# Half-width seven-product gate blocks in a two-layer transformer trunk: what one change does to its time

## The chip, the cores and the metric

The kernel runs on one core of one Trainium2 chip. The metric is the device time of one execution in microseconds (us). The engines named here are TensorE (PE: matrix products, with PEld for its weight loads), VectorE (DVE), ScalarE (ACT), GpSimd (POOL) and SyncE (SP, which issues the DMAs).

## The reference

256 tokens of width 2048 pass through two post-norm layers: layer 0 mixes by two kinds of 128-wide attention heads, layer 1 by latent attention. Each layer ends with a SwiGLU block of inner width 5632, which is where the change is:

```python
def swiglu(x, w_gate, w_up, w_down):
    return (jax.nn.silu(x @ w_gate) * (x @ w_up)) @ w_down
...
x = layer_norm(DEEPNORM_ALPHA * x + y, ln_g[layer, 0], ln_b[layer, 0])
y = swiglu(x, ffn_w_gate[layer], ffn_w_up[layer], ffn_w_down[layer])
```

All inputs and the output are float32.

## The kernel before, in words

**Products.** Every large product keeps float32 accuracy by splitting both factors into a high and a low part of type fp32r. `mm3` (L96) makes one product from three matmuls: high by high (L97), high by low weights (L98), low by high weights (L99). The activations are the stationary factor (128 rows of the contraction by 128 tokens), the weights are streamed, up to 512 columns to a matmul. Transposed activations lie in `XH`/`XL` (input of a product) and `YH`/`YL` (input of the output and down projections).

**Chunks, visits, pieces.** A *chunk* is an output block of 256 tokens by 512 columns; it sums in two PSUM banks, one for each half `t` of the tokens. A *piece* is 256 rows of the weights of one chunk (two contraction tiles `kk`), 512 KB. A *visit* is the use of one piece: `emit_visit` (L277) issues 2 `kk` x 2 `t` x 3 = 12 matmuls of 512 columns. The program is a list of visits built ahead by `kmajor`, `lead_begin`, `lead_end` and `ffn_part` (L177).

**Order of the work.** Every engine runs its own instructions in the order of the program text. For each visit the text issues the matmuls, then the evacuation of a finished chunk (`done`), then hooks tied to that visit (`at`), and then `feed_more` (L269).

**The feeder.** `feed_dma` (L231) issues the DMA of a piece into one of `NRAW` = 5 buffers `raw` on SP. `feed_split` (L244) makes its high part `wh` on ACT (L261) and its low part `wl = raw - wh` on DVE (L262), into one of `NW` = 9 pairs of buffers. A pair comes free at the last visit of its piece, so after each visit the split of the piece nine places on is issued; ACT waits there for PE to end the visit, DVE waits for ACT, and the `raw` buffer that comes free lets SP fetch another piece.

**FFN of a layer.** Eleven blocks `f` of 512 inner columns, in three groups (3, 4, 4 blocks). For each block the gate chunk `g` and the up chunk `u` (8 visits each). `g_done` (L758): Silu on ACT. `u_done` (L762): product on DVE. `h_T` (L765): four PE transposes for each half of the tokens, split into `YH`/`YL`. After a group, four down chunks `d`, each added to the residual on DVE (`residual`, L602). PSUM: four banks for chunks (`mm`), two for attention and some half chunks (`att`), two for transposes (`tp`).

**Between the mixer and the FFN** `setup_ln` (L707) runs the layer norm on DVE, ACT and POOL. The last chunk of the mixer and the first gate chunk visit five of their pieces one half of the tokens at a time to cover this. In layer 0 `toeplitz_prep` (L468) writes a bias table `t_d` of 1.5 MB on the same SP queue as the weights.

Of the kernel before, what the change touches and what calls it, by code (L numbers as in the profile page):

```python
# [9 lines left out]
F32 = mybir.dt.float32  # L10
# [11 lines left out]
NRAW = 5  # L22
NW = 9
# [10 lines left out]
class Chunk:  # L34
    """One GEMM output block: 2 token tiles x n columns, contracted over kt k-tiles."""

    def __init__(self, name, xs, kslots, subs, src, tags=("mm",)):
        self.name = name
        self.xs = xs
        self.kslots = kslots  # L40
        self.subs = subs
        self.src = src
        self.tags = tags
        self.nh = len(kslots) // 2
        self.n = sum(n for n, _ in subs) if subs else 0
        self.ps = {}
        self.subs_t, self.tags_t = {}, {}
        self.done = None


@with_exitstack
def trunk_kernel(ctx: ExitStack, tc: tile.TileContext, x, ab_w_in, b_f, ab_w_out,
# [35 lines left out]
    def ptile(tag):  # L88
        return psum.tile([P, 512], F32, name=uid(tag), tag=tag,
                         bufs={"mm": 4, "att": 2, "tp": 2}[tag])  # L90
# [10 lines left out]
    # ---------------------------------------------------------------- program  # L101
# [73 lines left out]
    GROUPS = ((0, 1, 2), (3, 4, 5, 6), (7, 8, 9, 10))  # L175

    def ffn_part(layer):  # L177
        for gi, grp in enumerate(GROUPS):
            for f in grp:
                for nm, w in (("g", w_gate), ("u", w_up)):  # L180
                    c = add_chunk(f"{nm}{layer}_{f}", "X", K16, ([512], lambda h, w=w, f=f: rows(
                        w[layer], h * 256, [(0, 512, f * 512)])))
                    if f == 0 and nm == "g":
                        lead_begin(c)
                    else:
                        kmajor(c)
            for n in range(4):
                c = add_chunk(f"d{layer}_{gi}_{n}", "Y", list(range(4 * len(grp))), (
                    [512], lambda h, b=grp[0] * 512, n=n: rows(
                        w_down[layer], b + h * 256, [(0, 512, n * 512)])))  # L190
                if gi == 2 and n == 3:
                    (lead_final if layer == 1 else lead_end)(c)
                else:
                    kmajor(c)

# [24 lines left out]
    # ----------------------------------------------------------------- feeder  # L220
# [8 lines left out]
    raws, wts = {}, {}  # L229

    def feed_dma(j, halves=False):  # L231
        if j >= len(pieces):
            return
        c, h = pieces[j]
        r = feed.tile([P, HPMAX], F32, name=uid("raw"), tag="raw", bufs=NRAW)
# [6 lines left out]
    whole = {}  # L242

    def feed_split(j, halves=False, part=None):  # L244
        if j >= len(pieces):
            return
        c, h = pieces[j]
        n = 2 * c.n
        if part != 1:
            r = raws.pop(j)  # L250
            wh = feed.tile([P, HPMAX], F32R, name=uid("wh"), tag="wh", bufs=NW)
            wl = feed.tile([P, HPMAX], F32R, name=uid("wl"), tag="wl", bufs=NW)
            wts[j] = (wh[:, :n].rearrange("p (k c) -> p k c", k=2),
                      wl[:, :n].rearrange("p (k c) -> p k c", k=2))
            whole[j] = (r, wh, wl)
        r, wh, wl = whole[j]
        cuts = [(0, c.n), (c.n, n)] if halves or part is not None else [(0, n)]
        if part is not None:
            cuts = [cuts[part]]
        for a, b in cuts:  # L260
            nc.scalar.activation(wh[:, a:b], r[:, a:b], AF.Copy)  # L261
            nc.vector.tensor_tensor(wl[:, a:b], r[:, a:b], wh[:, a:b].bitcast(F32),  # L262
                                    op=ALU.subtract)
        if part != 0:
            whole.pop(j)

    fs = {}

    def feed_more(lim):  # L269
        while fs["nsp"] < min(lim, len(pieces)):  # L270
            feed_split(fs["nsp"])
            fs["nsp"] += 1
            while fs["nd"] < len(pieces) and fs["nd"] - fs["nsp"] < NRAW:
                feed_dma(fs["nd"])
                fs["nd"] += 1

    def emit_visit(i):  # L277
        c, h, toks, *half = visits[i]
        j = pid[c.name, h]
# [16 lines left out]
    # ----------------------------------------------------- attention chains  # L296
# [57 lines left out]
    def transposes_r(srcs):  # L354
        tp = psum.tile([P, 512], F32R, name=uid("tpr"), tag="tp", bufs=2)
# [73 lines left out]
    # ------------------------------------------------------------- layer 0  # L429
# [143 lines left out]
    # --------------------------------------------------------- layer norm, FFN  # L573
    ff = {}

    def open_ffn(layer, src):
# [17 lines left out]
        at((f"{pre}2", 6, (0, 1)), lambda: load_b(layer, 0))  # L594

# [111 lines left out]
    def setup_ln(c3, nxt, final=False):  # L707
        """c3: chunk completing the sum; nxt: first chunk that reads the result."""
# [19 lines left out]
        def split_a():  # L728
            assert fs["nsp"] == p0 + 4
            feed_split(p0 + 4, part=0)  # L730
            fs["nsp"] += 1
# [20 lines left out]
    def ffn_done(layer):  # L752
        for gi, grp in enumerate(GROUPS):
            for li, f in enumerate(grp):
                cg, cu = chunks[f"g{layer}_{f}"], chunks[f"u{layer}_{f}"]
                hs = {}

                def g_done(t, cg=cg, hs=hs):  # L758
                    hs[t] = ff["pool"].tile([P, 512], F32, name=uid("s"), tag="s", bufs=4)
                    nc.scalar.activation(hs[t], cg.ps[t][0], AF.Silu)  # L760

                def u_done(t, cu=cu, hs=hs):  # L762
                    nc.vector.tensor_tensor(hs[t], hs[t], cu.ps[t][0], op=ALU.mult)

                def h_T(t, hs=hs, li=li):  # L765
                    tp = transposes([hs[t][:, k * P:(k + 1) * P] for k in range(4)])
                    sl = (slice(None), slice(4 * li, 4 * li + 4), slice(t * P, (t + 1) * P))
                    hilo(YH[sl], YL[sl], tp.rearrange("p (k c) -> p k c", k=4))

                cg.done, cu.done = g_done, u_done  # L770
                nx = (f"g{layer}_{f + 1}" if li + 1 < len(grp) else f"d{layer}_{gi}_0")
                at((nx, 1, (0, 1)), lambda h_T=h_T: h_T(0))
                at((nx, 2, (0, 1)), lambda h_T=h_T: h_T(1))
            for n in range(4):
                c = chunks[f"d{layer}_{gi}_{n}"]
                c.done = lambda t, half=None, c=c, n=n, gi=gi: residual(
                    c.ps[t], t, n, gi == 0, gi == 2,
                    fine=(layer == 1 and gi == 2 and t == 1), half=half)
# [6 lines left out]
    at(("u0_1", 0, (0, 1)), lambda: load_g(0, 1))  # L785
    at(("u0_1", 4, (0, 1)), lambda: load_b(0, 1))
# [5 lines left out]
    setup_ln(chunks["d0_2_3"], chunks["m0"])  # L792
# [4 lines left out]
    at(("m0", LEAD + 1, (0, 1)), lambda: (close_pool("ffn"), open_mla()))  # L797
    setup_ln(chunks["om3"], chunks["g1_0"])
    at(("u1_1", 0, (0, 1)), lambda: load_g(1, 1))
    at(("u1_1", 4, (0, 1)), lambda: load_b(1, 1))  # L800
    setup_ln(chunks["d1_2_3"], None, final=True)

    # ------------------------------------------------------------- layer 1
# [80 lines left out]
    for h in (5, 6, 7):  # L884
        hold["m2", h, (0, 1)] = pid["m2", 4] + NW + 1
# [90 lines left out]
    # ------------------------------------------------------------- emission  # L976
# [17 lines left out]
    warm = psum.tile([P, 512], F32, name="warm", tag="tp", bufs=2)  # L994
# [23 lines left out]
    for i, (c, h, toks, *half) in enumerate(visits):  # L1018
# [21 lines left out]
        if last_use[c.name, h] == i:  # L1040
            j = pid[c.name, h]
            if c.name == "v0" and h in (0, 2, 4):
                x_T(h + 2)
                feed_more(h + 3)
                x_T(h + 3)
            feed_more(min(j + NW + 1, i + 3 if i <= 4 else 8 + 17 * (i - 4) // 10, hold.get((c.name, h, toks), 10 ** 6)))
# [13 lines left out]
        if (c.name in ("oa1", "om1") and h == 6):  # L1060
            assert not chains, [(ch["head"], ch["stage"]) for ch in chains]
    close_pool("ffn")
# [57 lines left out]
```

## Time and profile before

| what | value |
|---|---|
| three runs | 2221.16, 2221.16, 2222.12 us; median 2221.16 us |
| span of the profiled execution | 2216.2 us (no other time is shown for it) |
| PE busy | 2182.8 us, 98% of the span |
| DVE, ACT, POOL busy | 1199.6 us (54%), 959.5 us (43%), 93.2 us (4%) |
| moved by DMA | 408.50 MB, mean 184 GB/s |

The span goes from the first to the last instruction of the profiled execution; the time of a run also holds what lies around it. Busy times of PE are those of overlapping instructions, so the pace of matmuls is read from the starts of one and the next.

### The profile page before, as it was taken

What the parts mean: (1) busy time and instruction counts of PE and PEld (TensorE: products, weight loads), DVE (VectorE), ACT (ScalarE), POOL (GpSimd) and SP (SyncE); (2) the same over time, 40 slices, a digit from 0 to 9 for tenths busy, and PEclk for the clock granted to TensorE, in tenths of its full rate; (3) what the DMA queues carried; (4) which work ended last, traced back from release to release, by engine and by line L of the source; (5) the groups of instructions that cost most, each with busy time, mean ns of one, the idle gap of its engine ahead of it and who ended that gap; (6) DMA issues with size and microseconds to landing.
All of it is one profiled execution on the core that took longest, in us unless ns stands there. A gap on an engine that the chain in (4) does not pass through costs nothing.

```text
span 2216.2 us, 26462 instructions
## 1 busy us (share of the span) xinstructions
PE 2182.8 (98%) x10134; PEld 1788.7 (81%) x10134; DVE 1199.6 (54%) x1443; ACT 959.5 (43%) x1232; POOL 93.2 (4%) x142
## 2 busy tenths in 40 slices
PE   9989999999999999999999999999999999999997
PEld 8768888888888888888888898888888888888886
DVE  6545556664544445445456677575454445444455
ACT  5444544354334443344433676344434443344441
POOL 2100000100000000000001321010000000000000
PEclk9989999999999999999999999999999999999999
DMA  8565655576566656666554644756565655665552
GB/s 286 136 185 153 180 173 188 182 239 224 184 188 188 182 181 189 190 184 187 180 184 148 207 127 134 265 172 226 180 189 183 187 183 187 186 188 181 189 184 74
DMA packets 229672, 408.50 MB, mean 184 GB/s; under 512 B 13961, under 2 KB 58025, under 8 KB 228521
## 3 DMA queue, kind: packets, MB, share of 16 engines
q1 hardware_dynamic: 229544, 406.81, 58.7%
q8 instruction: 79, 1.29, 0.2%
q14 instruction: 49, 0.39, 0.0%
HBM read 400.99 MB, written 5.77 MB: 184 GB/s over the span
## 4 chain that ended last, share of the span: by engine, by line
PE 96%; DMA 1%; DVE 1%; POOL 0%; ACT 0%; issue 0%; SPq 0%; DVEq 0%; ACTq 0%; POOLq 0%
PE mm L97 30%; PE mm L99 30%; PE mm L98 30%; PE tp L351 3%; DMA raw<-in_ab_w_in_dram 1%; PE att L98 1%; PE att L99 1%; PE att L97 1%; DVE X L669 0%; DVE X L663 0%; DMA xb<-in_x_dram 0%; ACT wh L261 0%; PE att L948 0%; PE att L949 0%; PE att L547 0%
## 5 line engine op out<-in xcount | busy, mean ns | idle before, releaser
L262 DVE TENSOR_TENSOR wl<-raw,wh 128x1024 fp32r<-128x1024 f32 (+3 forms) x748 | 899.1, 1206 | 814.8 <-ACT wh L261 810.8
L261 ACT ACTIVATE wh<-raw 128x1024 fp32r<-128x1024 f32 (+3 forms) x748 | 776.4, 1041 | 899.4 <-PE mm L99 830.2
L97 PE MATMUL mm<-wh,XH 128*128 128x512 f32 (+3 forms) x1984 | 785.6, 396 | 0.0
L99 PE MATMUL mm<-wh,XL 128*128 128x512 f32 (+3 forms) x1984 | 775.8, 391 | 0.0
L98 PE MATMUL mm<-wl,XH 128*128 128x512 f32 (+3 forms) x1984 | 773.8, 390 | 0.0
L99 PEld LDWEIGHTS mm<-wh,XL 128*128 128x128 f32 x1984 | 373.2, 188 | 84.4
L98 PEld LDWEIGHTS mm<-wl,XH 128*128 128x128 f32 x1984 | 373.9, 188 | 79.9
L97 PEld LDWEIGHTS mm<-wh,XH 128*128 128x128 f32 x1984 | 373.7, 188 | 79.4 <-ACT wh L261 0.2
L97 PE MATMUL mm<-wh,YH 128*128 128x512 f32 x960 | 380.1, 396 | 0.0
L99 PE MATMUL mm<-wh,YL 128*128 128x512 f32 x960 | 378.1, 394 | 0.0
L98 PE MATMUL mm<-wl,YH 128*128 128x512 f32 x960 | 377.0, 393 | 0.0
L99 PEld LDWEIGHTS mm<-wh,YL 128*128 128x128 f32 x960 | 180.2, 188 | 42.8
L98 PEld LDWEIGHTS mm<-wl,YH 128*128 128x128 f32 x960 | 180.4, 188 | 41.7
L97 PEld LDWEIGHTS mm<-wh,YH 128*128 128x128 f32 x960 | 180.4, 188 | 40.9
L658 POOL TENSOR_TENSOR mv<-mv,neghalf 128x1 f32<-128x1 f32 x8 | 7.6, 951 | 1832.1 <-DVE mv L657 1832.1
L93 ACT ACTIVATE YH<-tp 128x512 fp32r<-128x512 f32 x44 | 26.3, 598 | 85.0 <-PE tp L351 85.0
L94 DVE TENSOR_TENSOR YL<-tp,YH 128x512 fp32r<-128x512 f32 x44 | 30.4, 691 | 57.4 <-ACT YH L93 57.4
L93 ACT ACTIVATE XH<-tp 128x512 fp32r<-128x512 f32 x36 | 21.5, 597 | 72.5 <-PE tp L351 72.4
L760 ACT ACTIVATE s<-mm 128x512 f32<-128x512 f32 x44 | 26.1, 598 | 22.9 <-PE mm L99 20.7
L378 ACT ACTIVATE P<-P,sm 128x128 f32<-128x128 f32 x64 | 28.6, 449 | 16.7 <-DVE sm L368 16.7
L93 ACT ACTIVATE qkh<-tp 128x512 fp32r<-128x512 f32 x32 | 18.7, 597 | 37.7 <-PE tp L351 37.7
L94 DVE TENSOR_TENSOR qkl<-tp,qkh 128x512 fp32r<-128x512 f32 x32 | 21.7, 689 | 18.7 <-ACT qkh L93 18.7
(165 smaller groups left out, 962.3 us busy)
## 6 DMA issues: line engine op xcount, KB each, us to landing
raw<-in_ffn_w_gate_dram SPq DMA_DIRECT2D x176, 512.0 KB, 3.9
raw<-in_ffn_w_up_dram SPq DMA_DIRECT2D x176, 512.0 KB, 3.6
raw<-in_ffn_w_down_dram SPq DMA_DIRECT2D x176, 512.0 KB, 4.5
raw<-in_ab_w_in_dram SPq DMA_DIRECT2D x128, 256.0 KB, 3.2
raw<-in_ab_w_out_dram SPq DMA_DIRECT2D x32, 512.0 KB, 3.7
raw<-in_mla_w_out_dram SPq DMA_DIRECT2D x32, 512.0 KB, 3.9
raw<-in_ab_w_in_dram SPq DMA_DIRECT2D x24, 512.0 KB, 3.9
raw<-in_mla_w_ukv_dram SPq DMA_DIRECT2D x16, 512.0 KB, 3.6
```

The costliest lines, as they stand in the source:

```text
L93: nc.scalar.activation(hi, src, AF.Copy)
L94: nc.vector.tensor_tensor(lo, src, hi.bitcast(F32), op=ALU.subtract)
L97: nc.tensor.matmul(o, lh, rh, start=start, stop=False)
L98: nc.tensor.matmul(o, lh, rl, start=False, stop=False)
L99: nc.tensor.matmul(o, ll, rh, start=False, stop=stop)
L261: nc.scalar.activation(wh[:, a:b], r[:, a:b], AF.Copy)
L262: nc.vector.tensor_tensor(wl[:, a:b], r[:, a:b], wh[:, a:b].bitcast(F32), op=ALU.subtract)
L351: nc.tensor.transpose(tp[:, i * P:(i + 1) * P], s_, ident)
L378: nc.scalar.activation(pt[:, a:b], pt[:, a:b], AF.Exp, bias=sm[:, 2 + q:3 + q], accum_out=sm[:, 4 + q:5 + q])
L658: nc.gpsimd.tensor_tensor(mv[:, 3:4], mv[:, 2:3], neghalf, op=ALU.pow)
L760: nc.scalar.activation(hs[t], cg.ps[t][0], AF.Silu)
```

## The change

It touches the FFN of both layers, the feeder and the use of PSUM. Gates 1 to 10 of each layer become "S" chunks: their two halves of tokens, two contraction tiles of a piece and two halves of columns form a 2 x 2 by 2 x 2 block product, computed as seven block products of 128 x 128 by 128 x 256 in place of eight (a Strassen-Winograd scheme). Sums of activation blocks are made once per layer (`xs_batch`, four batches, into tiles `XS`); sums of weight blocks are made for each piece (`split_s`) in an enlarged raw buffer; the four results are put together when a gate chunk ends (`drain_s`). Gate 0 stays as it was.

```diff
-NRAW = 5
-NW = 9
+NR, NW = 4, 4
...
+    def s_window(on):
+        rot["mm"] = [0, 1, 7] if on else [0, 1, 2, 3]
+        rot["tp"] = [6] if on else [6, 7]
...
-    GROUPS = ((0, 1, 2), (3, 4, 5, 6), (7, 8, 9, 10))
+    GROUPS = ((0, 1), (2, 3), (4, 5), (6, 7), (8, 9, 10))
...
+        lead_begin(wide("g", w_gate, 0))
+        base = len(visits)
+        for f in range(NF):
+            kmajor(wide("u", w_up, f))
+            if f in (2, 4, 6, 8):
+                down(f // 2 - 1)
+        down(len(GROUPS) - 1)
+        flat = visits[base:]
...
+        for k, v in enumerate(flat):
+            visits.append(v)
+            want = (k - 3) * 0.85 if k < 22 else 16 + (k - 22) * 0.52
+            while ns < min(len(gates), want):
+                visits.append(gates[ns])
+                ns += 1
...
+    raw_free = [("N", feed.tile([P, HPMAX], F32, name=f"raw{i}")) for i in range(NR)]
+    raw_free += [("S", feed.tile([P, 2048], F32, name=f"sraw{i}")) for i in range(2)]
+    w_free = [("N", (feed.tile([P, HPMAX], F32R, name=f"wh{i}"),
+                     feed.tile([P, HPMAX], F32R, name=f"wl{i}"))) for i in range(NW)]
+    w_free += [("S", (feed.tile([P, 1792], F32R, name=f"sh{i}"),
+                      feed.tile([P, 1792], F32R, name=f"sl{i}"))) for i in range(2)]
...
+    def pay(keep=None):
+        for k, fn in list(owed):
+            if k != keep:
+                fn()
+        owed[:] = [x for x in owed if x[0] == keep]
+
+    def split_s(j):
+        r = raws.pop(j)
+        sh, sl = slot_of[j][1]
+        v = r.rearrange("p (q c) -> p q c", c=256)
+        nc.vector.tensor_tensor(v[:, 4:6], v[:, 0:1].broadcast_to([P, 2, 256]), v[:, 1:3],
+                                op=ALU.subtract)
+        nc.vector.tensor_tensor(v[:, 6], v[:, 1], v[:, 5], op=ALU.subtract)
+        nc.vector.tensor_tensor(v[:, 7], v[:, 3], v[:, 6], op=ALU.subtract)
+        nc.scalar.activation(sh, r[:, 256:2048], AF.Copy)
+
+        def lo():
+            nc.vector.tensor_tensor(sl, r[:, 256:2048], sh.bitcast(F32), op=ALU.subtract)
+            raw_free.append(rslot_of.pop(j))
...
+        owed.append((j, lo))
...
+            if c.S:
+                split_s(j)
+                pay(j)
+                return True
...
+    def emit_s(c, h):
...
+        for b, o, xt, q in (("A", 0, a(k0, 0), 0), ("A", 1, a(k1, 0), 2), ("D", 0, sf(1), 5),
+                            ("B", 0, sf(0), 3), ("B", 1, sf(2), 4), ("C", 0, sf(3), 1),
+                            ("C", 1, a(k1, 1), 6)):
+            mm_s(c.ps[b][:, o * 256:o * 256 + 256], xt, w, j, q, h == 0 and o == 0, h == c.nh - 1 and (o == 1 or b == "D"))
+
+    def drain_s(c, gt):
...
+        nc.scalar.activation(g11, A[:, 0:256], AF.Copy)
+        nc.vector.tensor_tensor(g22, g11, D[:, 0:256], op=ALU.add)
+        nc.vector.tensor_tensor(g11, g11, A[:, 256:512], op=ALU.add)
+        nc.vector.tensor_tensor(gx, v[:, 2:3].broadcast_to([P, 2, 256]),
+                                B.rearrange("p (l c) -> p l c", l=2), op=ALU.add)
+        nc.vector.tensor_tensor(g22, g21, B[:, 0:256], op=ALU.add)
+        nc.vector.tensor_tensor(gx, gx, C.rearrange("p (l c) -> p l c", l=2), op=ALU.add)
...
+    def xs_batch(n):
...
+        nc.vector.tensor_tensor(af.rearrange("p a b t c -> p (a b t c)"),
+                                XH[sl].rearrange("p k c -> p (k c)").bitcast(F32),
+                                XL[sl].rearrange("p k c -> p (k c)").bitcast(F32), op=ALU.add)
...
+        nc.vector.tensor_tensor(sf[:, :, 0], a21, a22, op=ALU.add)
+        nc.vector.tensor_tensor(sf[:, :, 1], sf[:, :, 0], a11, op=ALU.subtract)
+        nc.vector.tensor_tensor(sf[:, :, 2], a21, a11, op=ALU.subtract)
+        nc.vector.tensor_tensor(sf[:, :, 3], a12, sf[:, :, 1], op=ALU.subtract)
...
+        hilo(h_, l_, f_)
...
+        at((f"g{layer}_0", 5, (0, 1)), lambda: (xs_open(), xs_batch(0)))
+        for n in (1, 2):
+            at((f"g{layer}_0", 5 + n, (0, 1)), lambda n=n: xs_batch(n))
+        at((f"g{layer}_0", 7, (0, 1)), lambda: s_window(True))
+        at((f"u{layer}_0", 0, (0, 1)), lambda: xs_batch(3))
+        at((f"g{layer}_{NF - 1}", 7, (0, 1)), lambda: xs_close(layer))
```

`fetch` issues DMAs in the order of the pieces as long as a raw buffer of a fitting class is free; `feed_more` splits pieces in the same order as long as a pair of buffers of a fitting class is free. In the window of the S chunks, S pieces use the two "S" raw buffers and pairs and all others the four "N" ones; elsewhere a piece may take either class, and around the layer norms two more pairs ("X") that lie where `XS` is later. The low part of an S piece (`lo`) is issued behind the next split (`pay`). S chunks sum in the PSUM banks 2 to 5; other chunks of the window turn through banks 0, 1 and 7. `G` and `B` of the second layer norm are fetched by `xs_close`, after the last gate, instead of during `u_1`. The kernel is also built with `dynamic_dma_scratch_size=1024`.

## Rows read from the trace of the kernel before

**Rows 1.** Page: busy us of each engine (share of the span) xinstructions.
```profile
PE 2182.8 (98%) x10134; PEld 1788.7 (81%) x10134; DVE 1199.6 (54%) x1443; ACT 959.5 (43%) x1232; POOL 93.2 (4%) x142
```

**Rows 2.** Busy times in a stretch: us, five engines, PEclk, DMA share, GB/s.
```profile
465.20:1092.60 627.40, 627.40 (x2734) 505.81 (x2733) 307.36 (x279) 254.77 (x261) 0.00 (x0) 1.00 0.61 190
```

**Rows 3.** Waits by engine and line: us in total, times, longest us.
```profile
ACT wh L261 <- PE mm L99: 830.2, 493, 2.6
DVE wl L262 <- ACT wh L261: 810.8, 633, 17.0
```

**Rows 4.** Timeline of PE, 512 columns: start us, us; first and last of 49.
```profile
399.75 0.39 PE L97 MATMUL mm<-wh,YH 128*128 128x512 f32 x1
...
410.93 0.40 PE L97 MATMUL mm<-wh,YH 128*128 128x512 f32 x1
```

**Rows 5.** Timeline of PE, 256 columns, last chunk; first and last of 31.
```profile
2196.56 0.28 PE L97 MATMUL mm<-wh,YH 128*128 128x256 f32 x1
...
2200.10 0.28 PE L97 MATMUL att<-wh,YH 128*128 128x256 f32 x1
```

**Rows 6.** DVE by shape: xcount | busy us, mean ns | idle before.
```profile
L262 DVE TENSOR_TENSOR wl<-raw,wh 128x1024 fp32r<-128x1024 f32 x701 | 858.2, 1227 | 790.4 <-ACT wh L261 786.7 <-DMA raw<-in_ab_w_in_dram 1.4 <-DMA SIN<-in_cst_dram 1.2
...
L763 DVE TENSOR_TENSOR s<-s,mm 128x512 f32<-128x512 f32 x44 | 28.1, 680 | 0.0
...
L94 DVE TENSOR_TENSOR XL<-mm,XH 128x256 fp32r<-128x256 f32 x16 | 6.6, 422 | 2.7 <-ACT XH L93 1.6 <-PE mm L99 1.1
...
L262 DVE TENSOR_TENSOR wl<-raw,wh 128x512 fp32r<-128x512 f32 x6 | 4.1, 681 | 0.0
```

**Rows 7.** ACT by line and shape, columns as in Rows 6.
```profile
L261 ACT ACTIVATE wh<-raw 128x1024 fp32r<-128x1024 f32 x701 | 740.3, 1058 | 880.0 <-PE mm L99 827.6 <-DMA raw<-in_ab_w_in_dram 28.3 <-issue 11.2
...
L261 ACT ACTIVATE wh<-raw 128x512 fp32r<-128x512 f32 x6 | 3.7, 624 | 0.0
```

**Rows 8.** Timeline of DVE around the first layer norm of layer 0.
```profile
428.75 0.69 DVE L610 SCALAR_TENSOR_TENSOR X<-X,mm 128x512 f32<-128x512 f32 x1
429.47 0.69 DVE L614 BATCH_NORM_STATS2 st<-X 128x6 f32<-128x512 f32 x1
...
443.65 2.35 DVE L262 TENSOR_TENSOR wl<-raw,wh 128x1024 fp32r<-128x1024 f32 x2
...
448.25 6.05 DVE L262 TENSOR_TENSOR wl<-raw,wh 128x1024 fp32r<-128x1024 f32 x5
```

**Rows 9.** Timeline of DVE in the FFN of layer 0.
```profile
466.53 1.23 DVE L262 TENSOR_TENSOR wl<-raw,wh 128x1024 fp32r<-128x1024 f32 x1 [1.40 <-ACT wh L261]
```

**Rows 10.** Timeline of ACT in the FFN of layer 0.
```profile
459.40 2.96 ACT L261 ACTIVATE wh<-raw 128x1024 fp32r<-128x1024 f32 x3
...
465.44 1.06 ACT L261 ACTIVATE wh<-raw 128x1024 fp32r<-128x1024 f32 x1 [1.73 <-PE mm L99]
```

**Rows 11.** The chain that ended last, in order of time: transposes of one half.
```profile
482.20 0.44 PE tp L351 x4
```

**Rows 12.** Timeline of PE: the first matmul of the visit u0_0.4.
```profile
465.24 0.40 PE L97 MATMUL mm<-wh,XH 128*128 128x512 f32 x1
```

**Rows 13.** Timeline of ACT around a DMA wait in the attention of layer 0.
```profile
117.86 1.06 ACT L261 ACTIVATE wh<-raw 128x1024 fp32r<-128x1024 f32 x1 [19.22 <-DMA raw<-in_ab_w_in_dram]
```

**Rows 14.** Timeline of PE around the same wait.
```profile
106.57 0.39 PE L99 MATMUL mm<-wh,XL 128*128 128x512 f32 x1
120.72 0.87 PE L351 MATMUL tp<-ident,P 128*128 128x128 f32 x3 [13.77 <-DVE P L373]
```

**Rows 15.** Busy times in two stretches of layer 1, columns as in Rows 2.
```profile
1242.00:1246.00 4.00, 0.52 (x5) 0.34 (x3) 2.39 (x3) 1.12 (x3) 3.84 (x6) 1.00 0.95 330
1246.00:1250.00 4.00, 3.89 (x13) 3.16 (x14) 0.96 (x1) 1.64 (x3) 3.69 (x9) 0.70 0.42 114
```

**Rows 16.** DMA issues by line: xcount, KB each, median us to landing.
```profile
raw<-in_ffn_w_gate_dram SPq DMA_DIRECT2D x176, 512.0 KB, 3.9
...
G<-in_ln_g_dram SPq DMA_DIRECT2D x4, 1024.0 KB, 6.1
```

More of the change, by code (lines that the diff above doesn't have):

```diff
@@ L173, in w_out_part, with wide, down @@
         lead_end(cs[3])
-    GROUPS = ((0, 1, 2), (3, 4, 5, 6), (7, 8, 9, 10))
+    GROUPS = ((0, 1), (2, 3), (4, 5), (6, 7), (8, 9, 10))
+    NF = 11
+    after_up = {}
+    win = {}
     def ffn_part(layer):
[L178 to L186, printed above, removed]
+        def wide(nm, w, f):
+            return add_chunk(f"{nm}{layer}_{f}", "X", K16, ([512], lambda h: rows(
+                w[layer], h * 256, [(0, 512, f * 512)])))
+        def down(gi):
+            grp = GROUPS[gi]
+            slots = [4 * (f % 4) + k for f in grp for k in range(4)]
             for n in range(4):
[L188 to L191, printed above, removed]
+                c = add_chunk(f"d{layer}_{gi}_{n}", "Y", slots, (
+                    [512], lambda h, n=n: rows(
+                        w_down[layer], grp[0] * 512 + h * 256, [(0, 512, n * 512)])))
+                if gi == len(GROUPS) - 1 and n == 3:
                     (lead_final if layer == 1 else lead_end)(c)
@@ L194, in ffn_part @@
                     kmajor(c)
+        lead_begin(wide("g", w_gate, 0))
[6 more added lines that the diff above has]
+        flat = visits[base:]
+        del visits[base:]
+        for f in range(NF):
+            e = max(k for k, v in enumerate(flat) if v[0].name == f"u{layer}_{f}")
+            after_up[layer, f] = [(v[0].name, v[1], v[2]) for v in flat[e + 2:e + 4]]
+        gates = []
+        for f in range(1, NF):
+            c = wide("g", w_gate, f)
+            c.S = True
+            gates += [(c, h, (0, 1)) for h in range(8)]
+        ns = 0
+        for k, v in enumerate(flat):
[4 more added lines that the diff above has]
+                ns += 1
+        assert ns == len(gates)
     w_out_part("oa", ab_w_out[0])
@@ L249, in feed_split @@
         if part != 1:
+            got = take(w_free, j) if j in raws else None
+            if got is None:
+                return False
+            slot_of[j] = got
+            if c.S:
+                split_s(j)
+                pay(j)
+                return True
             r = raws.pop(j)
-            wh = feed.tile([P, HPMAX], F32R, name=uid("wh"), tag="wh", bufs=NW)
-            wl = feed.tile([P, HPMAX], F32R, name=uid("wl"), tag="wl", bufs=NW)
+            wh, wl = got[1]
             wts[j] = (wh[:, :n].rearrange("p (k c) -> p k c", k=2),
@@ L265, in feed_split, with fetch @@
             whole.pop(j)
+            raw_free.append(rslot_of.pop(j))
+        pay()
+        return True
     fs = {}
+    def fetch():
+        while fs["nd"] < len(pieces) and feed_dma(fs["nd"]):
+            fs["nd"] += 1
     def feed_more(lim):
-        while fs["nsp"] < min(lim, len(pieces)):
-            feed_split(fs["nsp"])
+        fetch()
+        while fs["nsp"] < min(lim, len(pieces)) and feed_split(fs["nsp"]):
             fs["nsp"] += 1
-            while fs["nd"] < len(pieces) and fs["nd"] - fs["nsp"] < NRAW:
-                feed_dma(fs["nd"])
-                fs["nd"] += 1
+            fetch()
@@ L752, in ffn_done, with g_done, u_done, h_T @@
     def ffn_done(layer):
[L753 to L773, printed above, removed]
+        for f in range(NF):
+            cg, cu = chunks[f"g{layer}_{f}"], chunks[f"u{layer}_{f}"]
+            def g_done(t, cg=cg, f=f):
+                gt = ff["gt"][f % 2]
+                if not cg.S:
+                    nc.scalar.activation(gt[:, t], cg.ps[t][0], AF.Silu)
+                elif t == 1:
+                    drain_s(cg, gt)
+                    g_ = gt.rearrange("p t c -> p (t c)")
+                    nc.scalar.activation(g_, g_, AF.Silu)
+            def u_done(t, cu=cu, f=f):
+                h_ = ff["gt"][f % 2][:, t]
+                nc.vector.tensor_tensor(h_, h_, cu.ps[t][0], op=ALU.mult)
+            def h_T(t, f=f):
+                h_ = ff["gt"][f % 2][:, t]
+                tp = transposes([h_[:, k * P:(k + 1) * P] for k in range(4)])
+                y = 4 * (f % 4)
+                sl = (slice(None), slice(y, y + 4), slice(t * P, (t + 1) * P))
+                hilo(YH[sl], YL[sl], tp.rearrange("p (k c) -> p k c", k=4))
+            cg.done, cu.done = g_done, u_done
+            for t in (0, 1):
+                at(after_up[layer, f][t], lambda h_T=h_T, t=t: h_T(t))
+        last = len(GROUPS) - 1
+        for gi in range(len(GROUPS)):
             for n in range(4):
@@ L992, in x_T @@
         return evac() if now else evac
[L994 removed]
+    warm = ptile("tp")
     load_x(0, 0)
```

147 lines of the change are left out of this document (125 added, 22 removed).

## The prediction

> **What bounds the kernel now.** I read the page's busy times first: PE is busy for 98% of the span, DVE for 54%, ACT for 43% [rows 1]. Then the busy times of one stretch, from the visit u0_0.4 to the end of the last up chunk of layer 0: PE covers all of its 627.40 us, DVE only 307.36 [rows 2]. Then the waits: ACT waits for PE for 830.2 us in total, and DVE for ACT for 810.8 [rows 3]. So the feeder has time to spare, each split waits for PE to free a pair of buffers, and time is set by the pace of matmuls. Both views also show the order that matters below: DVE takes its instructions in the order of the text and stands still while the next one waits, whatever lies behind it.
>
> **Fewer columns on PE.** 49 matmuls of 512 columns start 11.18 us apart from first to last, so one costs 11.18 / 48 = 0.233 us, and a visit of twelve 2.795 us [rows 4]. 31 matmuls of 256 columns, with a weight load each as in the new blocks, take 3.54 / 30 = 0.118 us each [rows 5]. An S visit of 7 x 3 = 21 is then 2.48 us. It saves 0.317 us, and 160 gate pieces save 50.7 us, as long as PE stays the bound.
>
> **What DVE and ACT get in return.** A piece now costs DVE one low part of 1024 columns, 1.23 us [rows 6]. An S piece costs it three subtractions (512, 256 and 256 columns) and a low part of 1792; ACT copies 1792 columns in place of 1024. The rows give 0.68 us for 512 and 0.42 for 256 on DVE [rows 6]. For 1792 no row exists. From 512 to 1024 columns DVE grows by 0.546 us [rows 6] and ACT, from 0.624 to 1.058, by 0.434 [rows 7]; one and a half times this on top of 1024 gives 2.05 us and 1.71 us. The bounds are the cost of 1024 itself (1.23, 1.06) and 1.75 times it (2.15, 1.85); I take the extrapolation, since two rows lie on its line.
>
> [...]
>
> **The cycle of the feeder.** This term decides. Nine pairs of split buffers and five raw ones become six of each, in the window two for S pieces and four for N pieces (all others). After an S visit one S pair is free, so the text issues, in this order: on DVE the three subtractions; on ACT the copy `sh`; on ACT the copy `wh` of the next N piece; on DVE its `wl`; on DVE the deferred low part of the S piece. `sh` needs the subtractions, `wh` stands behind `sh` on ACT, `wl` needs `wh`, and the low part and the next subtractions stand behind `wl` on DVE. It is one chain through two queues. Gaps: a DVE instruction that reads the result of the one before starts 0.03 us after its end, independent ones overlap by 0.1 (two of 1.22 in 2.35) [rows 8]. DVE starts 0.03 us after ACT ends (465.44 + 1.06, then 466.53) [rows 9, 10], and ACT overlaps copies by 0.1 (three in 2.96) [rows 10]. So:
> subtractions 0.68 + 0.03 + 0.42 + 0.03 + 0.42 = 1.58; to ACT 0.03; `sh` 1.71; `wh` 0.96; to DVE 0.03; `wl` 1.23; low part 1.95; overlap with the next -0.08. Together 7.4 us for an S piece and one N piece.
>
> The window holds 80 S visits and 141 others in a layer, so 0.76 more N pieces per cycle, at 1.13 us each on DVE [rows 8]: 0.86 us. DVE also empties PSUM, by 0.60 us for each 512 columns back to back [rows 6]: per layer 20 for ups, 20 low parts behind transposes, 32 residual additions (16 down chunks in the window, more than before because of five groups) and 10 gate drains of 3 x 0.42 + 2 x 0.68 = 2.6; 69 us, 0.87 per cycle. The sum is 9.1. I take 9.0, since a drain that falls into DVE's wait for ACT costs nothing; at the ends all drains fall there (8.3) or none do and the gate drains wait for ACT's first copy too (9.4).
>
> PE itself needs 2.48 + 1.76 x 2.795 + 0.11 (transposes, 0.44 for a half [rows 11]) = 7.5 us per cycle, and before the same work took 7.83. So DVE's chain becomes the bound. PE will wait mostly at the start of chunks, where with three banks in place of four the second half needs a bank that DVE has yet to empty, and at S visits for their low part.
>
> **Entry into the window.** Each of four `xs_batch` is a chain too: 1.23 + 4 x 0.45 on DVE, 1.06 on ACT, 1.23 on DVE and gaps, 5.4 us. DVE gets to the first at about 449.5, after two of the five splits of [rows 8]; with two N splits between, the fourth ends at 473.4 and u0_0.4 is split at 474.6, where PE wanted it at 465.24 [rows 12]: a wait of 9.4 us. The first S piece follows through the chain: subtractions to 476.2, copies to 478.9, `wl` to 480.1, low part to 482.1.
>
> **Sum for a layer.** From 482.1, 79 more cycles of 9.0 us end at 1193, and the last S visit at 1195.5. Before, PE is through the same 222 visits at 465.24 + 222 x 2.795 + 18 x 0.44 = 1093.6. The layer loses 102 us, both lose 204. What follows (some 30 visits without S pieces) is bound by PE again and costs the same.
>
> **Smaller parts.** (1) Fewer pairs outside the window. In the attention of layer 0 ACT stands 19.22 us on a weight piece that is fetched behind the table write, with work for heads behind it in the queues [rows 13], and PE loses 14 us [rows 14]. With six pairs the piece in question is split a visit later, and what PE lacks then is a later step of a head: it gets two more visits, 5.6 us, done before it stands. I take 6 us of gain; the ends are 0 and the whole 14. In the entry of layer 1 PE's one wait, 3.5 us in [rows 15], may vanish or double; I take none. (2) `G` and `B` fetched later, behind the last gate on SP's queue: 6.1 us for `G` [rows 16] beside some 30 visits of 2.8 us of cover; pieces behind them have six raw buffers and six pairs, 33 us. Nothing, or, without that cover, 13 us per layer. (3) S raw buffers: a fetch takes 3.9 us [rows 16] against a cycle of 9 until its subtractions. Nothing. (4) The scratch size for dynamic DMA: no row shows it. ACT waits for a fetch of weights for 28.3 us in all [rows 7]; I take nothing, with that as the end on either side.
>
> **Forecast.** The span is 2216.2 us, and the median of the runs 5.0 us longer, which I carry over. 2221.2 + 204 - 6 = 2419; I say 2420 us. A measurement of this kernel can tell about 0.2% (4.4 us) from no change.
>
> **Rivals.** *PE stays the bound.* If DVE does not stand still for `sh` and `wh` (2.70 us a cycle), because other work lies there, its cycle is 6.3 us, below PE's 7.5. The point of decision is 1.5 us of that chain. Then 2221.2 - 50.7 - 6 = 2165, or 2193 with both entries. For it: the busy time alone fits. Against: nothing in the text's order comes between, and [rows 13] shows a queue that stands although work behind it is ready. 0.13.
> *The clock falls as well.* [...] 0.07. [...]
> *All drains hide*, 8.3 us a cycle: 2310; this lies in the forecast's own range, as does 9.4 us (2480).
> *Nothing changes in effect*, since the gain on PE and the chain cancel (a cycle of 7.7): 0.03.
>
> **How the numbers follow.** The forecast with its ends has 0.77, the clock 0.07, so slower has 0.84, faster 0.13, no change 0.03. The range from 2290 to 2490 holds the drains' ends and the clock; a tenth of the slower cases, the even one and the faster one are left out.
>
> **What would show it.** Right: in the window DVE's gaps before `wl` are put down to ACT's copies of 1792 and 1024; low parts of 1792 take about 2.05 us; an S cycle takes about 9 us; PE's waits name DVE, 100 us a layer or more, mostly before first matmuls of chunks; S matmuls keep 0.118 us. Wrong: PE without gaps in the window, or DVE doing drains or `wl` while ACT copies.

## The result, and the profile after

The changed kernel takes **2449.09 us** (median of 4 runs, 2448.76 to 2450.24), the kernel before, beside it, 2221.16 us: a ratio of 1.1028 with a 95% interval from 1.1012 to 1.1044. I had said 2420 us, in a range from 2290 to 2490, slower with a chance of 0.84.

Page of the changed kernel: busy times, and from the costliest groups the split of an N piece and the two long operations of an S piece.
```profile
PE 2221.0 (91%) x11562; PEld 1874.1 (77%) x11562; DVE 1631.5 (67%) x2103; ACT 1050.1 (43%) x1240; POOL 93.0 (4%) x142
...
L374 DVE TENSOR_TENSOR wl<-raw,wh 128x1024 fp32r<-128x1024 f32 (+4 forms) x431 | 521.6, 1211 | 502.6 <-ACT wh L373 499.5
L341 ACT ACTIVATE sh<-sraw 128x1792 fp32r<-128x1792 f32 x160 | 272.2, 1701 | 714.2 <-DVE sraw L340 651.9
...
L344 DVE TENSOR_TENSOR sl<-sraw,sh 128x1792 fp32r<-128x1792 f32 x160 | 323.0, 2019 | 0.0
```
No engine is full any more. PE is idle for 2447.4 - 2221.0 = 226 us, against 33 before [rows 1], and DVE, which got 432 us more work, still rests for a third of the span. Where no engine is full, I look for a chain, and the groups suggest its links: idle time of 499.5 us before DVE's `wl` ended when ACT had made `wh`, and 651.9 us before ACT's `sh` when DVE had made the sums. Two engines wait for each other.

Waits of the changed kernel by engine and line: us in total, times, longest us.
```profile
ACT sh L341 <- DVE sraw L340: 651.9, 149, 6.4
DVE wl L374 <- ACT wh L373: 524.7, 266, 7.1
ACT wh L373 <- PE mm L110: 118.9, 68, 7.3
...
PE mm L108 <- DVE gt L979: 91.5, 22, 7.6
PE mm L108 <- DVE X L824: 42.8, 17, 6.0
PE sA L397 <- DVE sl L344: 22.5, 13, 3.8
```
The wait that told that the feeder had time to spare, ACT for PE, has gone from 830.2 us [rows 3] to 118.9. PE's longest waits name DVE: `gt` and `X` are banks that DVE has not emptied yet, `sl` is a low part that is not there.

DVE's wait for ACT was even longer before, 810.8 us [rows 3], so its total proves nothing by itself: there ACT in turn waited for PE. The same waits in the FFN of layer 0 alone, of the kernel before (465.2 to 1092.6 us):
```profile
ACT wh L261 <- PE mm L99: 322.5, 191, 1.8
```
and of the changed kernel (475 to 1205 us):
```profile
DVE wl L374 <- ACT wh L373: 205.0, 81, 7.1
...
ACT wh L373 <- PE mm L110: 5.5, 2, 3.5
```
DVE now waits about once for each of the 80 S pieces, and ACT is hardly held by PE.

Timeline of DVE in layer 0, one cycle: start us, us, what, and the idle time before it.
```profile
763.81 0.69 DVE L337 TENSOR_TENSOR sraw<-sraw 128x512 f32<-128x512 f32 x1
764.53 0.42 DVE L339 TENSOR_TENSOR sraw<-sraw 128x256 f32<-128x256 f32 x1
764.99 0.42 DVE L340 TENSOR_TENSOR sraw<-sraw 128x256 f32<-128x256 f32 x1
768.27 1.23 DVE L374 TENSOR_TENSOR wl<-raw,wh 128x1024 fp32r<-128x1024 f32 x1 [2.85 <-ACT wh L373]
769.41 2.02 DVE L344 TENSOR_TENSOR sl<-sraw,sh 128x1792 fp32r<-128x1792 f32 x1
771.35 1.22 DVE L374 TENSOR_TENSOR wl<-raw,wh 128x1024 fp32r<-128x1024 f32 x1
772.48 0.68 DVE L337 TENSOR_TENSOR sraw<-sraw 128x512 f32<-128x512 f32 x1
```
Timeline of ACT, the same cycle.
```profile
765.59 1.70 ACT L341 ACTIVATE sh<-sraw 128x1792 fp32r<-128x1792 f32 x1 [0.59 <-DVE sraw L340]
767.19 1.99 ACT L373 ACTIVATE wh<-raw 128x1024 fp32r<-128x1024 f32 x2
774.25 1.70 ACT L341 ACTIVATE sh<-sraw 128x1792 fp32r<-128x1792 f32 x1 [5.07 <-DVE sraw L340]
```
Read the two side by side. DVE ends the sums at 765.41, ACT copies `sh` and the first `wh` (765.59 to 768.2), and DVE stands for 2.85 us although `sl` of this S piece could have been made from 767.3 on: it lies behind `wl` in DVE's queue. In layer 0 the idle time of DVE there is this 2.85 us in 60 of 80 cycles; in 17 DVE empties a bank (`X`, `YL` or `gt`) within the wait. Then DVE works through `wl`, `sl`, `wl`, and ACT stands for 5.07 us until the next sums. The cycle is 772.48 - 763.81 = 8.67 us with one extra N piece and no drain in it. Over layer 0 the first `sl` starts at 475.0 and the 80th at 1195.4: 9.12 us a cycle.

Timeline of PE: the longest kind of wait, and the first and last of the 21 matmuls of an S visit.
```profile
561.36 0.40 PE L110 MATMUL mm<-wh,XL 128*128 128x512 f32 x1
567.68 0.80 PE L108 MATMUL mm<-wh,XH 128*128 128x512 f32 x1 [5.93 <-DVE gt L979]
...
1202.52 0.28 PE L396 MATMUL sA<-sh,XH 128*128 128x256 f32 x1
...
1204.87 0.28 PE L398 MATMUL sC<-sh,XL 128*128 128x256 f32 x1
```
21 matmuls start within 2.35 us, so one still costs 0.118 us, and the visit 2.47. The products are as cheap as forecast; they are just not fed.

Busy times of two stretches of the changed kernel, columns as in [rows 2].
```profile
565.00:569.00 4.00, 1.32 (x3) 1.12 (x4) 3.96 (x6) 0.00 (x0) 0.00 (x0) 0.54 0.46 138
569.00:573.00 4.00, 4.00 (x17) 3.32 (x17) 1.12 (x3) 2.65 (x2) 0.00 (x0) 0.60 0.32 124
```
These are the last 2.7 us of the wait of 5.93 us and the 5.3 us of work behind it. PE's granted clock is 0.54 and 0.60 in them, and 0.50 from 569.2 to 571 us, where matmuls of 512 columns start 0.43 us apart in place of 0.233 [rows 4], though PE is busy without a gap in the second stretch.

### The profile page after: what moved, and what is told of

Read it like the earlier page. It is cut to its first block, busy times and chain, and to the rows that moved or that the text cites. A ratio compares the mean times of both kernels' runs of the same rounds, so it can differ in the third digit from the quotient of the medians.

```text
span 2447.4 us, 29962 instructions
## 1 busy us (share of the span) xinstructions
PE 2221.0 (91%) x11562; PEld 1874.1 (77%) x11562; DVE 1631.5 (67%) x2103; ACT 1050.1 (43%) x1240; POOL 93.0 (4%) x142
## 4 chain that ended last, share of the span: by engine, by line
PE 43%; issue 40%; DVE 11%; ACT 3%; DMA 1%; POOL 1%; SPq 0%; ACTq 0%; DVEq 0%; POOLq 0%
PE mm L108 12%; PE mm L109 11%; PE mm L110 11%; DVE sl L344 4%; DVE wl L374 2%; ACT wh L373 2%; PE tp L510 2%; ACT sh L341 1%; DMA sraw<-in_ab_w_in_dram 1%; DVE sraw L337 1%; PE att L109 1%; PE att L110 1%; PE att L108 1%; DVE sraw L339 1%; DVE sraw L340 1%
## 5 line engine op out<-in xcount | busy, mean ns | idle before, releaser
L374 DVE TENSOR_TENSOR wl<-raw,wh 128x1024 fp32r<-128x1024 f32 (+4 forms) x431 | 521.6, 1211 | 502.6 <-ACT wh L373 499.5
L341 ACT ACTIVATE sh<-sraw 128x1792 fp32r<-128x1792 f32 x160 | 272.2, 1701 | 714.2 <-DVE sraw L340 651.9
L108 PE MATMUL mm<-wh,XH 128*128 128x512 f32 (+3 forms) x1100 | 448.6, 408 | 70.5 <-DVE gt L979 45.6
L373 ACT ACTIVATE wh<-raw 128x1024 fp32r<-128x1024 f32 (+4 forms) x431 | 439.2, 1037 | 147.8 <-PE mm L110 79.5
L109 PE MATMUL mm<-wl,XH 128*128 128x512 f32 (+3 forms) x1100 | 439.2, 399 | 2.1 <-DVE wl L374 2.1
L110 PE MATMUL mm<-wh,XL 128*128 128x512 f32 (+3 forms) x1100 | 437.4, 398 | 0.0
L108 PE MATMUL mm<-wh,YH 128*128 128x512 f32 (+1 forms) x768 | 318.4, 415 | 85.7 <-DVE gt L979 46.0
L344 DVE TENSOR_TENSOR sl<-sraw,sh 128x1792 fp32r<-128x1792 f32 x160 | 323.0, 2019 | 0.0
L109 PE MATMUL mm<-wl,YH 128*128 128x512 f32 (+1 forms) x768 | 312.9, 407 | 0.0
L110 PE MATMUL mm<-wh,YL 128*128 128x512 f32 (+1 forms) x768 | 311.5, 406 | 0.0
L397 PE MATMUL sA<-sl,XH 128*128 128x256 f32 x320 | 94.2, 294 | 22.5 <-DVE sl L344 22.5
```

The source lines that it names most:

```text
L108: nc.tensor.matmul(o, lh, rh, start=start, stop=False)
L109: nc.tensor.matmul(o, lh, rl, start=False, stop=False)
L110: nc.tensor.matmul(o, ll, rh, start=False, stop=stop)
L341: nc.scalar.activation(sh, r[:, 256:2048], AF.Copy)
L344: nc.vector.tensor_tensor(sl, r[:, 256:2048], sh.bitcast(F32), op=ALU.subtract)
L397: nc.tensor.matmul(o, h, w[1][:, q], start=False, stop=False)
```

## The experiments

The theory that the timelines suggest: the pace is a chain of sums, `sh`, `wh`, `wl`, `sl`, through DVE's and ACT's queues in the order of the text. Its rivals: the clock or PE itself; the banks and groups that came with the change; loads; plain busy time, whatever the order.

**E1: swap the copies.** ACT copies the next N piece's `wh` ahead of `sh`, where the split of that piece is issued together with the S piece's. (`copies` issues the `sh` that is owed; its definition and its other calls are left out here.)
```diff
-        nc.scalar.activation(sh, r[:, 256:2048], AF.Copy)
+        owed_sh.append(lambda: nc.scalar.activation(sh, r[:, 256:2048], AF.Copy))
...
             nc.scalar.activation(wh[:, a:b], r[:, a:b], AF.Copy)
+            copies()
```


> ACT copies the next N piece before the S piece, so that copy runs while DVE makes the subtractions, and DVE does not wait for two copies in a row. Chain theory: a cycle falls from 9.1 us to PE's own 7.5, DVE's gaps before low parts shrink from about 2.7 us a cycle to about 0.5, and the time is 2200 to 2260 us. Clock theory (the halved TensorE clock and TensorE's own work set the time): no more than 40 us lower, over 2400. Bank theory (three PSUM banks and four N pairs are too few, whatever the split costs): over 2400 as well.

Measured: 2347.95 us, 1.0571 (1.0555 to 1.0586). 101 us came back by a reordering alone, but the 2200 to 2260 us that I expected was too low. Timeline of DVE of E1 in the later part of layer 0:
```profile
746.07 0.42 DVE L350 TENSOR_TENSOR sraw<-sraw 128x256 f32<-128x256 f32 x1
749.35 1.23 DVE L385 TENSOR_TENSOR wl<-raw,wh 128x1024 fp32r<-128x1024 f32 x1 [2.85 <-ACT wh L383]
```
The wait is the old 2.85 us. By the order of the text no pair is free for the next N piece when the S piece is split in this part (the four N pairs hold the four N pieces ahead), so there is nothing to copy first, and the trace of ACT has `sh` ahead of `wh` here. In the first 16 cycles, where S and N pieces alternate, the cycle fell from 8.27 to 6.47 us; in the others from 9.33 to 9.04.

**E2: the first sum made twice** (512 columns on DVE).
```diff
+        nc.vector.tensor_tensor(v[:, 4:6], v[:, 0:1].broadcast_to([P, 2, 256]), v[:, 1:3],
+                                op=ALU.subtract)
```


> The subtraction of 512 columns (0.69 us on DVE) is made twice for each of the 160 S pieces. Chain theory: each adds its whole length to the cycle, 160 x 0.69 = 110 us, 2550 to 2570 us. Clock theory: DVE has gaps, nothing is added, 2449 +- 10. Bank theory: the drains come later by part of it, 2450 to 2500.

Measured: 2569.2 us, 1.1568 (1.1545 to 1.1591): 120 us more, or 0.75 us for each of 160 S pieces. The second one starts 0.72 us behind the first (0.685 us and a gap), so nearly all of it reaches the end. The sums lie on the path. An engine bound by its busy time alone would show the same; E9 tells these two apart.

**E3: product D made twice** (three more matmuls in each S visit, 57 us of PE; the gates' values change).
```diff
+                            ("D", 0, sf(1), 5),
```


> Block product D is made twice in each S visit, three more matmuls of 256 columns, 0.354 us for each of 160 visits, 57 us of TensorE time (the gates 1 to 10 hold one product twice, so that their values differ). Chain theory: TensorE has gaps of over 100 us a layer and takes most of it there: 2450 to 2470 us. Clock theory: the whole 57 us or more, 2505 or above. Bank theory: 2450 to 2480.

Measured: 2450.19 us, 1.1032 (1.101 to 1.1054), 1 us more for 57 us of work. Busy times in a stretch of layer 0, of the changed kernel:
```profile
560.00:1180.00 620.00, 547.49 (x2939) 465.68 (x2939) 432.13 (x495) 254.59 (x225) 0.00 (x0) 0.94 0.49 164
```
and of E3:
```profile
560.00:1180.00 620.00, 564.98 (x3134) 485.45 (x3134) 434.20 (x497) 252.51 (x223) 0.00 (x0) 0.96 0.49 163
```
DVE and ACT do what they did and PE fills its gaps. So PE's time in the S visits is not on the path. The granted clock rose as the gaps were filled, from 0.94 to 0.96 here, and PE's busy time over the whole span rose by 41 us and not by 57. E3 does not hold the clock fixed, then, but 41 us of busy PE left 1 us in the time. The rival that PE itself sets the pace falls, and with the granted clock at 0.94 to 0.96 there was still room for the added work in the time in which PE waits anyway.

**E4: plain gates in the new order.** Order of visits, banks, five groups and split buffers of the change; the gates are products of 512 columns.
```diff
-            c.S = True
+            c.W = True
...
+        if c.W and h == 0:
+            b0 = 2 + 2 * (int(c.name.split("_")[1]) % 2)
+            c.ps = {t: [bank(b0 + t, "w")] for t in (0, 1)}
```


> Gates 1 to 10 are plain products of 512 columns again, without sums of blocks; the interleaving with up and down pieces, five down groups, the banks (three in turn, four for the gates), the raw buffers and the pairs stay as changed. Chain theory: DVE needs 1.23 us for each visit of 2.8 and keeps up, so about the time of the kernel before less the 6 us in the attention, 2210 to 2235 us. Bank theory: most of the loss stays, over 2350. Clock theory: like the kernel before, as TensorE does not wait, 2215 to 2235.

Measured: 2214.27 us, 0.9969 (0.9957 to 0.9982). The order, the banks, the groups and the buffers are harmless, or 0.3% better than before. The 235 us lie in what E4 leaves out: the S pieces and how they are fed, with the sums of activations and the drains of the gates.

**E5: late low part.** `sl` is issued behind the next S piece's sums, where DVE stood.
```diff
             raw_free.append(rslot_of.pop(j))
-        pay()
         return True
```


> Edit: the low part of an S piece is no longer issued right behind the next normal split, but only behind the next S piece's subtractions (or when its visit comes, if that is sooner). No instruction is added or taken away; on VectorE the order subtractions, wl, low part becomes low part of the last S piece, subtractions, wl, so that VectorE has 2.02 us of ready work where it waited for ScalarE. Chain theory: the chain of one S piece (subtractions 1.58, sh 1.70, wh 0.96, wl 1.23, low part 2.02) loses the low part, 7.5 down to 5.5 us, and with the 0.86 and 0.87 us of the other splits and the drains to about 7.2, under the 7.5 us that TensorE needs: TensorE sets the pace again but for the chunk starts. 160 S pieces x (9.12 - 7.6 to 7.9) = 195 to 240 us less where the whole cycle is followed; as some S pieces still come back to back, I take 160 to 185: 2265 to 2290 us, VectorE's wait wl <- wh well under the 524.7 us of the changed kernel, and mean distance of low parts about 8.0 us. Buffer theory (rival): an S raw buffer is now held for one more piece, there are only two, and the load of the next S piece takes 4 to 6 us: the subtractions wait for DMA instead, gain under 60 us, 2390 or more, with a VectorE wait on sraw put down to the DMA queue. Sum theory (rival: VectorE's own busy time and ScalarE's copies are the pace, order does not matter): 2440 to 2450.

**E6: E1 and E5 together.**

> Edit: the late low part of E5 and the swapped copies of E1 together (ScalarE copies the next normal split ahead of the long S copy, where that split has been issued). Chain theory: the wl of VectorE then waits for subtractions' 0.96 us of wh alone where the swap bites, but the late low part has already taken most of that wait; only the cycles in which the low part came too late gain again, some 0.1 us each: 10 to 20 us under E5, 2250 to 2275. If the two edits each took away their own wait, the gains would add: 2449 - 101 - 170 = 2178, below the kernel before. If the late low part alone uses all of the slack (TensorE is the pace everywhere but at starts): equal to E5 within 5 us.

Measured: E5 2333.39 us, 1.0511 (1.0491 to 1.0531); E6 2328.43 us, 1.049 (1.0472 to 1.0507). E5 gives back 116 us and not 160 to 185. E6 is 5 us under E5, no more than E5's own runs lie apart (2328 to 2338 us): the case for which I had said "equal to E5 within 5 us". Waits of E5:
```profile
ACT sh L341 <- DVE sraw L340: 487.6, 147, 6.1
DVE wl L374 <- ACT wh L373: 325.9, 311, 6.2
...
DVE sraw L337 <- DMA sraw<-in_ffn_w_gate_dram: 75.9, 62, 3.0
...
PE sA L396 <- DVE sl L344: 72.5, 50, 5.3
```
Two new waits stand in the place of the old. DVE now waits for loads, as the buffer theory said: `sl` frees the raw buffer, and a late `sl` makes a late load. And PE waits for `sl` itself (22.5 us before). The time stays under the 2390 us of that theory. So the low part late is better where S pieces are far apart (cycles after the 16th: 8.64 us, against 9.04 in E1 and 9.33 in the changed kernel), and not as good as E1 where they are dense (7.73 against 6.47).

**E7: E6 with the S visits laid evenly.**
```diff
-            want = (k - 3) * 0.85 if k < 22 else 16 + (k - 22) * 0.52
+            want = (k - 2) * 0.8 if k < 22 else 16 + (k - 22) * 0.5
```


> Edit: E6, and the S visits laid more evenly: from the 2nd visit behind gate 0 at 0.8 a visit (was from the 3rd at 0.85), and behind the 22nd visit exactly one S visit after every second normal one (0.5 in place of 0.52), so that two S pieces seldom come back to back and the last S visit is not early. Same instructions, another order. Chain theory: where two S pieces come back to back with one normal piece between them the chain has to make two S splits in the time of 2.48 + 2.8 us of TensorE; without such places only the entry to each FFN (10 to 20 us) and the gate boundaries are left: 10 to 30 us per layer under E6, 2205 to 2240. If the spacing does not matter (mean rates decide): equal to E6 within 5 us. Below 2214 it beats the kernel before and E4 too, and the two-queue chain was all that kept the half-width products from paying; if it stays over 2221, something else (entry, drains, clock) still costs as much as the 101 us of TensorE time that the products save.

Measured: 2272.05 us, 1.0239 (1.0224 to 1.0255), again above what I expected, though spacing alone gave 56 us. Where the rest lies can now be read from PE, since little else is left. From the layer norm ahead of layer 0's FFN to the one behind it (the second and the third instruction of layer-norm statistics, L656 before and L879 here, from start to start) E7 takes 775.2 us, and PE's own work in it is 80 x 2.48 + 184 x 2.795 + 22 x 0.44 = 722 us. From the 17th S visit to the last but one PE has hardly a gap. The 53 us are at the entry (14.3 us), in the first 16 S visits (some 20), at and behind the last one (10), and the rest half a microsecond each at the first visits of gates. Timeline of DVE there, among the first S pieces:
```profile
489.03 0.69 DVE L347 TENSOR_TENSOR sraw<-sraw 128x512 f32<-128x512 f32 x1 [2.83 <-DMA sraw<-in_ffn_w_gate_dram]
...
490.56 2.02 DVE L354 TENSOR_TENSOR sl<-sraw,sh 128x1792 fp32r<-128x1792 f32 x1
...
496.51 0.69 DVE L347 TENSOR_TENSOR sraw<-sraw 128x512 f32<-128x512 f32 x1 [1.33 <-DMA sraw<-in_ffn_w_gate_dram]
```
and of PE, which waits for that `sl`:
```profile
492.63 0.39 PE L408 MATMUL sA<-sl,XH 128*128 128x256 f32 x1 [1.96 <-DVE sl L354]
```
Here gates 1 and 2 must be done before ups 1 and 2, so 16 S visits share 22 normal ones; there are two raw buffers for S pieces, and in this density their loads are late.

**E8: a later, thinner start.** Gates 1 and 2 plain, as in E4; the four `xs_batch` behind visits 1, 3, 5 and 7 of up 0; `sl` at once where no S piece is among the next three.
```diff
-            c.S = True
+            c.S, c.W = f > 2, f <= 2
...
+        if not any(isS[j + 1:j + 4]):
+            pay()
...
-        at((f"g{layer}_0", 5, (0, 1)), lambda: (xs_open(), xs_batch(0)))
-        for n in (1, 2):
-            at((f"g{layer}_0", 5 + n, (0, 1)), lambda n=n: xs_batch(n))
+        at((f"g{layer}_0", 5, (0, 1)), xs_open)
+        for n in range(4):
+            at((f"u{layer}_0", 2 * n + 1, (0, 1)), lambda n=n: xs_batch(n))
```


> Edit, on E7: gates 1 and 2 are plain 512-column products (in the half-width chunks' banks), so that the half-width gates 3 to 10 come at one S visit for two normal ones from the start; the four batches that make the sums of x are issued behind visits 1, 3, 5 and 7 of up 0 instead of behind gate 0's last visits; the low part of an S piece with no other S piece among the next three is issued at once. What it should take away is what E7's trace of layer 0 still shows as TensorE's waits: 14.3 us before the first half-width chunk, some 20 us in the first 16 S visits (waits of 0.5 to 2.3 us for the low part sl, where S visits stand at 0.8 to a normal one), 4.4 us at the last S visit and 3.8 us and a half-clock stretch behind it, 46 us in all of the 53 us by which the stretch from LN1 to LN2 (775.2 us) is over TensorE's own matmuls. What it gives back: 16 plain visits at 2.80 in place of 2.48 us, 5 us. Chain theory: 775 - 35 to 43 + 5 = 737 to 745 us per FFN against 744.6 of the kernel before, so 2192 to 2212 us with the 6 us of the attention's down-stream gain; ratio 0.987 to 0.996. If the half-width products cost something that no chain shows (clock, banks, a slower steady visit): the steady part stays as it is in E7 and the time stays over 2221.

**E9: E8 with the change's order in the two queues.** The same instructions; `sh` first on ACT, `sl` behind the next N split on DVE.
```diff
-        owed_sh.append(lambda: nc.scalar.activation(sh, r[:, 256:2048], AF.Copy))
+        nc.scalar.activation(sh, r[:, 256:2048], AF.Copy)
...
-        if not any(isS[j + 1:j + 4]):
-            pay()
+        pay()
```


> E8 with the order of the change put back in the two queues alone: the long S copy first on ScalarE, the low part behind the next normal split on VectorE. Same instructions, same visits of TensorE. Chain theory: a steady S cycle is set by the chain again, 9.1 to 9.3 us against TensorE's 8.1 to 8.3 in this spacing: 2 x 64 x 0.9 to 1.1 = 115 to 140 us over E8, 2310 to 2350. If with this spacing TensorE hides the order (each S piece has two normal visits to be made ready in): within 20 us of E8.

Measured: **E8 2199.26 us, 0.9892 (0.9872 to 0.9911)**, faster than the kernel before and than E4; E9 2363.23 us, 1.0638 (1.0617 to 1.0659). One of E8's four executions took 6485 us, and what it was I don't know. The median of 2199.26 counts it; the ratio leaves it out (2198.07 us without it). E8 holds three edits on top of E7, and what each is worth alone was not measured; between E8 and E9 the order is the only difference. Page of E8, busy times:
```profile
PE 2155.6 (98%) x11274; PEld 1821.6 (83%) x11274; DVE 1562.0 (71%) x1987; ACT 1034.2 (47%) x1240; POOL 93.0 (4%) x142
```
Waits of PE in E8, us in total, times, longest us:
```profile
PE mm L108 <- DVE gt L995: 10.0, 2, 5.0
PE sA L410 <- DVE sl L354: 7.4, 16, 1.9
```
Page of E9, busy times:
```profile
PE 2215.9 (94%) x11274; PEld 1858.5 (79%) x11274; DVE 1552.0 (66%) x1987; ACT 1029.3 (44%) x1240; POOL 93.1 (4%) x142
```
Waits of PE in E9, columns the same:
```profile
PE mm L108 <- DVE gt L994: 59.6, 18, 5.0
...
PE mm L108 <- DVE X L839: 44.4, 18, 3.2
```
The counts on PE, DVE and ACT are the same in both, and so is the work of each instruction; only their order in two queues differs, and the time by 164 us. PE's granted clock is lower in E9 (0.965 against 0.994 over the span), but PE is idle for 146 us there, so the clock alone does not make the difference. An S cycle in layer 0 takes (1161.1 - 558.5) / 63 = 9.57 us in E9 and (1081.4 - 564.9) / 63 = 8.20 in E8, where PE needs 2.48 + 2 x 2.795 + 0.11 = 8.18: PE is the bound again. Timeline of DVE in E8, one cycle:
```profile
704.20 0.69 DVE L347 TENSOR_TENSOR sraw<-sraw 128x512 f32<-128x512 f32 x1
704.92 0.42 DVE L349 TENSOR_TENSOR sraw<-sraw 128x256 f32<-128x256 f32 x1
705.38 0.42 DVE L350 TENSOR_TENSOR sraw<-sraw 128x256 f32<-128x256 f32 x1
705.73 2.02 DVE L354 TENSOR_TENSOR sl<-sraw,sh 128x1792 fp32r<-128x1792 f32 x1
708.66 1.22 DVE L385 TENSOR_TENSOR wl<-raw,wh 128x1024 fp32r<-128x1024 f32 x1 [0.91 <-ACT wh L383]
```
Behind the sums there is now the `sl` of the S piece before, ready to run while ACT copies, and the wait of 2.85 us is down to 0.91. The stretch from layer norm to layer norm is 1166.3 - 428.9 = 737.4 us, against 744.6 before, and PE's own work in it 64 x 2.48 + 200 x 2.795 + 10 = 727 us.

## Why the prediction was right

**The chain through two queues** was the term that decided, and it held: 9.12 us a cycle where I took 9.0. Its links measure 0.685 + 2 x 0.425 us for the sums, 1.70 for `sh`, 2.02 for `sl`, and the wait of `wl` for `wh` is there as worked out: DVE ready at 765.4, `wl` at 768.27. I had extrapolated 1.71 and 2.05 us from two rows each; the trace has 1701 and 2019 ns. E2 shows the sums on the path, E9 against E8 that the order makes the pace, not the busy time.

**The products on PE** cost 2.47 us a visit, forecast 2.48. The gain of 50.7 us was there and could not be used: E3 hid 57 us more of matmuls.

**The sum for a layer** was too small: 102 us, where the stretch between the layer norms grew by 862.1 - 744.6 = 117.5 us in layer 0 and 861.93 - 743.25 = 118.7 in layer 1. Of layer 0 three terms were mis-sized and one was left out. 79 cycles at 0.12 us more are 9.5. The last S visit ends 7.6 us behind its low part (1197.4 to 1205.0), where I had 2.5, since normal visits and a wait of 1.6 us for a bank lie between: 5.1. The first low part ended at 477.0 and not at 482.1, of which 3 us only follow the earlier layer norm: -2. And behind the last S visit one wait for a bank costs 1.1 us, where I had nothing. Together 13.7 of 15.5 us; where the other 1.8 us lie is not shown.

**PE's waits** name DVE, and stand mostly at the first matmuls of chunks, as said. The size was near: those of the list above and the shorter ones come to some 190 us for both layers, 95 a layer, just under the 100 or more that I had asked for.

**The attention** gave less than 6 us: PE's one wait went from 13.8 us [rows 14] to 6.05 and 0.77, but PE lost 1 us in its start, and the 1800th matmul came 4.2 us earlier, the layer norm 3.1. Another 1.7 us went behind the waits, where PE works without gaps at a granted clock of 0.63 (124 to 130 us; before, 0.80 from 121 to 130): that fits the lower clock, but no run shows it by itself. That six pairs of buffers were the reason was argued from the order and isn't tested alone; E4, which has them too, shows a gain of the same kind.

**The time around the span** was read wrongly. The runs list time and span side by side, and they lie 1.8 us apart in the changed kernel (2449.25 and 2447.4) and in the kernel before (2222.8 and 2221.0 in one run beside E7). The 5.0 us that I carried over set the median of some runs against the span of another, which was some 3 us quicker than that median. So the spans of the two profiles lie 231.2 us apart, and the medians 227.9.

**The rivals.** PE as the bound needed 1.5 us of the chain to hide; in the change's order only some emptying of banks hid, in 17 of 80 cycles. E8, with 128 S pieces of 160, comes to 2199 us, near the 2193 of this rival: its condition, other work in DVE's wait, is what E5 and E8 put there. The clock fell, as the second rival has it (0.54 and 0.60 above), but no run shows what a lower clock by itself costs in the window, for which the prediction has the chance of 0.07 and a share of the range. What the runs show is that the changed kernel, at a mean granted clock of 0.957, took 57 us more of matmuls in E3 for 1 us: while DVE and ACT set the pace, a slower PE has time. Ahead of the window, where nothing hides it, the clock may have cost the 1.7 us above, an estimate that no run shows by itself.

**The expectations** of E1, E5, E6 and E7 were all too hopeful, mostly for one reason: I used one mean cycle for a stretch with two densities. Where S and N pieces alternate, the swap helps and a late `sl` meets the loads; where they are apart, the swap finds no N piece to put first and the late `sl` helps. E2, E3, E4 and E8 came out within what I had said; E9 was missed on the other side, by 13 us.

## What to carry to other kernels

Where work is cut so that one engine needs less, follow one piece through all queues in the order of the text, and add up the links: two engines at 67% and 43% can be the bound of a third. Then look at what lies behind each waiting instruction: if it is ready, move it ahead; in E8's spacing this was worth 164 us of 2363 without an instruction less. A late release had its price at the other end, in the load that waits for the buffer (DVE's idle time before the first sums, 0.0 us in the changed kernel, was 75.9 us of waits for loads in E5), so look at the densest stretch by itself, not at means.

## What the runs showed of the hardware

In the changed kernel PE had room for its stretches at a lower clock: the mean granted clock is 0.957, and 57 us of matmuls added in E3 (clock 0.966) made it 1 us longer. No cost of weight loads shows in the short matmuls: 256 columns with a load each started 0.118 us apart before [rows 5], after (21 starts within 2.35 us), and in E7 (21 starts from 715.58 to 717.93 us), half of the 0.233 us of 512 columns [rows 4], also next to visits of 512 columns. On DVE the 64 low parts of layer 0 in E8 took 2015 to 2021 ns each.
